# Turning queries and keys in 32x32 blocks by VectorE and transfers, instead of by TensorE, in the attention layer of a hybrid DiT

## The chip, the core and the metric

One core of one Trainium2 chip runs the whole program. The time is the device time of one execution in microseconds (us), the median of several executions. Engines are named as the profile names them: PE is TensorE (matmuls; PEld its weight loads), DVE is VectorE, ACT is ScalarE, POOL is GpSimd, SP is SyncE, which only starts transfers here.

## The reference

Two layers, 256 tokens and 256 context tokens, width 2048, float32. Layer 0 mixes by a Fourier branch; layer 1 is attention with 64 query heads on 8 kv heads of 64, a window of 128, context keys, axial rotary embedding of queries and keys, and a sink in each softmax:

```python
h = _rmsnorm(x, norm_g[i]) * (1 + scale) + shift
...
q, k, v, z = jnp.split(h @ w_in, [D_BRANCH, D_BRANCH + kvw, D_BRANCH + 2 * kvw], axis=-1)
kc, vc = jnp.split(hc @ w_in[:, D_BRANCH:D_BRANCH + 2 * kvw], 2, axis=-1)
...
q = _axial_rope(q.reshape(b, n, ATTN_Q_HEADS, ATTN_HEAD_DIM), rows, cols)
k = _axial_rope(k.reshape(b, n, ATTN_KV_HEADS, ATTN_HEAD_DIM), rows, cols)
...
s = jnp.einsum('bqhgd,bkhd->bhgqk', q, k).astype(jnp.float32) * (ATTN_HEAD_DIM ** -0.5)
...
p = jax.nn.softmax(jnp.concatenate([s, sk], axis=-1), axis=-1)[..., :-1]
return jnp.einsum('bhgqk,bkhd->bqhgd', p.astype(v.dtype), v)
...
y = jnp.moveaxis(o, 0, 1).reshape(b, n, D_BRANCH) * jax.nn.silu(z)
...
x = x + gate * (y @ w_out[i])
return _rmsnorm(x, final_g)
```

For the scores, queries and keys must stand with the 64 elements of a head in the partitions, while the projections and the rotary embedding leave them with tokens in the partitions. So they have to be turned. This turning is what the change is about.

## The kernel before

**Arithmetic.** A float32 product is made of three passes over rounded halves (`mm3`, L79 to L81): high by high, high by low, low by high. Each piece of weights, 128x1024, is cast by ACT to its high half (`w_cast`, L1119, `wh`), and DVE subtracts it from the original to get the low half (`w_low`, L1125, `wl`). The text calls the second "a low". SP's queue loads weights (L47, `raw`, 128x2048, three buffers); a load waits until the DVE has read the buffer that it takes.

**Units.** What the attention layer still has to project is cut into 142 units of 1024 weight columns: eight for the queries of each kv head, eight for its z, and fourteen for steps of the output projection. Units of the next head's queries, z and output are placed between the steps of the attention itself, so that PE has work while softmax runs.

**The attention loop.** 64 iterations, eight for each kv head; PE, DVE and ACT keep the order in which the code issues. One iteration i: DVE takes the masked maximum of the scores (`s_max`, L1215, two halves) and turns the probabilities of iteration i-1 in 32x32 blocks (`x_turn`, L1245, into `pall`); a unit goes to PE; ACT does the exponentials (L1224, L1225, `es`), then what has come due (`posts`), then the cast of a later unit; DVE and ACT divide by the sums (L1230, L1231, L1233); DVE makes a low; PE makes the scores of iteration i+1 (L1206, L1207); then come DVE's parts of what has come due (`rests`), and a second unit with its low and its cast. At every eighth iteration, PE multiplies the probabilities of the eight iterations behind it with v (`stage_o`, L1252, 256 matmuls in two halves, with a unit between them); it reads all of `pall`, so it needs the last x_turn. DVE then weights the result with z (`emit_y`, L1261), and GpSimd's queue loads v for the next head (`load_v`, L1242). A round is the stretch from one stage_o to the next; there are seven stage_o in the loop, and so six full rounds, a first one from the loop's start, and a last one.

**Turning before.** The keys, `kr`, 128 tokens x 512 by four, are turned ahead of the loop by sixteen PE transposes (L971) and copied by ACT (L973) to `kT`. The queries of heads 1 to 7: when the last unit of a head's queries is done, at the fourth iteration of the round before, ACT copies them out of PSUM (`finish_q`, L1031), GpSimd applies the rotary embedding (`roped`, L912, L917 twice, L918, for each of two blocks of tokens), and PE turns a pair of heads with four transposes (`q_turn`, L1048), one pair in the sixth iteration and the other in the seventh. An iteration later ACT casts the turned pair to its high half (`q_cast`, L1054, L1055) and DVE makes its low half (L1058, L1059), both from PSUM. A pair p2 = 0 serves the first four iterations of a head, p2 = 1 the last four. The high and low halves of a head's keys are made in the fifth iteration of the round before (`prep_kk`: ACT L1018 twice, `kkh`; GpSimd L1020 twice, `kkl`, the "k subtraction"). Of head 0, queries and keys are made ahead of the loop.

Of the kernel before, what the change touches and what calls it, by code (L numbers as in the profile page):

```python
# [10 lines left out]
F32 = mybir.dt.float32  # L11
# [18 lines left out]
def tile_dit(ctx: ExitStack, tc: tile.TileContext, a: dict, out: bass.AP):  # L30
# [888 lines left out]

    with tc.tile_pool(name="h1", reuse_waits="tile", bufs=16) as h1p:  # L920
        hx1 = []
        kT = []
        with tc.tile_pool(name="kvp", reuse_waits="tile", bufs=2) as kvp:
# [33 lines left out]
            for tb in range(4):  # L957
                t = kvp.tile([P, 512], F32, tag="v", name="v", bufs=4)
                S.copy(t, o[tb][1])
                for g in range(4):  # L960
                    nc.gpsimd.dma_start(vd[:, :, tb * 4 + g, :].rearrange("h j d -> j h d"), t[g * 32 : g * 32 + 32].rearrange("p (h d) -> p h d", d=64))
# [5 lines left out]
                kr.append(t)  # L967
            for hp in range(4):
                o = psum()
                for tb in range(4):  # L970
                    PE.transpose(o[:, tb * P : (tb + 1) * P], kr[tb][:, hp * P : (hp + 1) * P], ident)  # L971
                t = act()
                S.copy(t, o)  # L973
                kT.append(t)
# [5 lines left out]
        with tc.tile_pool(name="ye", reuse_waits="tile", bufs=6) as yep, ExitStack() as ats:  # L980
# [28 lines left out]
            now, posts, rests, turns = [-1], [], [], {}  # L1009

            def prep_kk(hk):
                kkh = at.tile([P, 512], F32R, tag="kkh", name="kkh")
                kkl = at.tile([P, 512], F32R, tag="kkl", name="kkl")
                b = (hk % 2) * 64
                src = kT[hk // 2][b : b + 64, :]
                with tc.issue_after(kk_hold[0]) if hk < 2 else nullcontext():
                    for c in (0, 64):
                        S.copy(kkh[c : c + 64, :], src)  # L1018
                for c in (0, 64):
                    (GP if hk else V).tensor_tensor(kkl[c : c + 64, :], src, kkh[b : b + 64, :].bitcast(F32), op=ALU.subtract)  # L1020
                kk[hk] = (kkh, kkl)

            def finish_q(hk, oq):
                qr = []
                for tb in range(2):
                    t = act()
                    if hk == 0:
                        roped(t, oq[tb], tb, actp, "act")
                    else:
                        t0 = act()  # L1030
                        S.copy(t0, oq[tb])  # L1031
                        roped(t, t0, tb, actp, "act", GP)
                    qr.append(t)
                if now[0] < 0:
                    prep_kk(hk)
                    for p2 in range(2):
                        defer.append(lambda p2=p2: q_cast(hk, p2, q_turn(p2, qr)))
                else:
                    posts.append((now[0] + 1, lambda: prep_kk(hk)))
                    for p2 in range(2):  # L1040
                        turns[now[0] + 2 + p2] = lambda p2=p2: (hk, p2, q_turn(p2, qr))
# [9 lines left out]
            def q_cast(hk, p2, o):  # L1051
# [10 lines left out]
                second(low)  # L1062
# [200 lines left out]
            for i in range(10):  # L1263
# [15 lines left out]
            with tc.manual_schedule(engines=engines):  # L1279
# [7 lines left out]
                for i in range(64):  # L1287
                    now[0], m = i, share[i % 8] + (i > 61 or i == 2)
# [6 lines left out]
                    run(posts)  # L1295
                    w_cast(pos[0] + 2)
# [4 lines left out]
                    run(rests)  # L1301
                    if i % 8 == 0 and i:
# [16 lines left out]
                    if i in turns:  # L1319
                        args = turns.pop(i)()  # L1320
                        posts.append((i + 1, lambda args=args: q_cast(*args)))
# [228 lines left out]
```

## Time and profile before

| What | Value |
|---|---|
| Median of 3 executions | 1769.63 us (1769.47 to 1773.46) |
| The profiled execution's own time | 1769.88 us |
| Its span, first to last instruction | 1768.1 us, granted TensorE clock 0.998 |
| Busy: PE / PEld / DVE / ACT / POOL | 99 / 84 / 78 / 50 / 10% |
| One round of the loop (1251.0 to 1311.0) | 60.0 us |
| PE transposes of the queries (L1048) / of the keys (L971) | 64 / 16 |

Times in rows are us from the span's start, then the duration; groups give the sum of busy time in us, the mean of one in ns, and the idle time ahead of them. Instructions on PE overlap, so what one costs is read from the start of one to the start of the next. A row like "[0.58 <-ACT wh L1119]" is idle time of the engine just before that instruction, and what ended it. DVE's group L1125 carries 130 lows from 1131 to 1612, about the loop (mean 1.36 us) and L1119 the casts ahead of them (mean 1.05 us). DVE and ACT instructions overlap a little with their neighbours too, by about 0.1 us.

### The profile page before, as it was taken

Reading aid. Unit: us, or ns where it says so; the run is one execution under the profiler, and the core shown is the slowest. Engines: PE = TensorE matmul, PEld = TensorE weight load, DVE = VectorE, ACT = ScalarE, POOL = GpSimd, SP = SyncE. Lnnn points to the kernel's source line nnn. Section 1 sums busy time; section 2 is a strip of 40 time slices with the busy share of each in tenths; the row PEclk is TensorE's granted clock in tenths of the full one; section 3 lists DMA queues with packets and bytes.
Section 4 is the critical chain, followed back from the end, with each engine's and each line's share of the span. In section 5 each row is a group of like instructions: output and inputs, shape, how many; then the busy total and the mean of one; then the engine's idle time right before and its main releaser. Section 6 shows DMA issues by size and latency. Waiting matters only on the chain.

```text
span 1768.1 us, 28034 instructions
## 1 busy us (share of the span) xinstructions
PE 1754.8 (99%) x10967; PEld 1480.5 (84%) x10967; DVE 1377.2 (78%) x2318; ACT 878.1 (50%) x1522; POOL 184.5 (10%) x223
## 2 busy tenths in 40 slices
PE   9999999999999999999999999999999999999998
PEld 7669999998888888888888888888888888887886
DVE  6769999978897887587986473798889888987455
ACT  6545444543222232333332352687778777876343
POOL 0001000020000010000000001133123302301000
PEclk9999999999999999999999999999999999999999
DMA  9994655476766777654566333544444444446553
GB/s 389 422 381 167 210 206 207 167 274 226 304 255 247 262 275 266 259 208 156 207 240 236 113 142 108 188 146 156 155 153 147 139 148 156 146 159 235 197 183 141
DMA packets 69108, 370.20 MB, mean 209 GB/s; under 512 B 8816, under 2 KB 11008, under 8 KB 35440
## 3 DMA queue, kind: packets, MB, share of 16 engines
q1 hardware_dynamic: 55600, 328.63, 50.5%
q0 software_dynamic: 9488, 32.95, 5.5%
q10 hardware_dynamic: 3888, 6.83, 1.1%
q8 instruction: 86, 1.41, 0.3%
q14 instruction: 46, 0.38, 0.1%
HBM read 353.16 MB, written 15.21 MB: 208 GB/s over the span
## 4 chain that ended last, share of the span: by engine, by line
PE 97%; ACT 1%; DVE 1%; DMA 0%; issue 0%; SPq 0%; DVEq 0%; ACTq 0%
PE ps L79 26%; PE ps L81 26%; PE ps L80 26%; PE ps L1177 7%; PE ps L1175 3%; PE ps L1252 3%; PE ps L347 2%; PE ps L1207 2%; PE ps L1206 2%; PE ps L1048 0%; DMA xn<-in_x 0%; PE ps L662 0%; PE ps L628 0%; PE ps L363 0%; DVE wl L1125 0%
## 5 line engine op out<-in xcount | busy, mean ns | idle before, releaser
L69 ACT CAST wh<-raw 128x1024 fp32r<-128x1024 f32 x178 | 186.9, 1053 | 402.9 <-PE ps L80 345.2
L70 DVE TENSOR_TENSOR wl<-raw,wh 128x1024 fp32r<-128x1024 f32 x178 | 219.8, 1235 | 137.9 <-ACT wh L69 137.8
L80 PE MATMUL ps<-hx,wh 128*128 128x512 f32 x700 | 272.6, 389 | 0.0
L79 PE MATMUL ps<-hx,wh 128*128 128x512 f32 x700 | 271.1, 390 | 0.0
L81 PE MATMUL ps<-hx,wl 128*128 128x512 f32 x700 | 271.1, 390 | 0.0
L1125 DVE TENSOR_TENSOR wl<-raw,wh 128x1024 fp32r<-128x1024 f32 x142 | 191.2, 1352 | 56.5 <-ACT wh L1119 56.0
L1119 ACT CAST wh<-raw 128x1024 fp32r<-128x1024 f32 x142 | 148.8, 1048 | 70.9 <-PE ps L80 58.2
L699 DVE CUSTOM_DVE_ANT_0 raw<-raw,cb 128x1024 f32<-128x1024 f32 x128 | 155.0, 1220 | 35.5 <-DMA raw<-in_adw 34.7
L79 PEld LDWEIGHTS ps<-hx,wh 128*128 128x128 f32 x700 | 131.4, 188 | 27.9 <-ACT hx L432 0.8
L81 PEld LDWEIGHTS ps<-hx,wl 128*128 128x128 f32 x700 | 131.5, 188 | 27.2
L80 PEld LDWEIGHTS ps<-hx,wh 128*128 128x128 f32 x700 | 131.5, 188 | 27.2
L699 DVE CUSTOM_DVE_ANT_0 junk<-raw,cb 128x1024 f32<-128x1024 f32 x96 | 117.2, 1221 | 27.4 <-DMA raw<-in_adw 14.1
L1177 PE MATMUL ps<-h,wh 128*128 128x512 f32 x512 | 127.3, 391 | 0.0
L79 PE MATMUL ps<-wh,h 128*128 128x512 f32 x320 | 124.9, 397 | 0.2 <-ACT h L932 0.2
L80 PE MATMUL ps<-wl,h 128*128 128x512 f32 x320 | 124.9, 390 | 0.0
L81 PE MATMUL ps<-wh,h 128*128 128x512 f32 x320 | 124.6, 391 | 0.0
L1224 ACT ACTIVATE p<-ps,mx 128x512 f32<-128x512 f32 x128 | 86.8, 683 | 52.9 <-DVE mx L1215 52.8
L1177 PEld LDWEIGHTS ps<-h,wh 128*128 128x128 f32 x512 | 94.2, 188 | 18.1
L1215 DVE CUSTOM_DVE_ANT_0 ps<-ps,mask,nsink 128x512 f32<-128x512 f32 x128 | 91.1, 752 | 0.5
L80 PE MATMUL ps<-act,wh 128*128 128x512 f32 x234 | 91.0, 389 | 0.0
L81 PE MATMUL ps<-act,wl 128*128 128x512 f32 x234 | 90.3, 390 | 0.3 <-DVE wl L70 0.3
L79 PE MATMUL ps<-act,wh 128*128 128x512 f32 x234 | 89.7, 389 | 0.0
(362 smaller groups left out, 3959.8 us busy)
## 6 DMA issues: line engine op xcount, KB each, us to landing
raw<-in_adw SPq DMA_DIRECT2D x64, 1024.0 KB, 4.9
raw<-in_wz SPq DMA_DIRECT2D x58, 1024.0 KB, 4.8
raw<-in_awp SPq DMA_DIRECT2D x32, 1024.0 KB, 12.4
raw<-in_wo SPq DMA_DIRECT2D x32, 1024.0 KB, 4.8
raw<-in_wq SPq DMA_DIRECT2D x32, 1024.0 KB, 4.7
raw<-in_wu SPq DMA_DIRECT2D x25, 1016.0 KB, 5.0
raw<-in_wo1b SPq DMA_DIRECT2D x16, 1024.0 KB, 4.8
act<-in_xT POOLq DMA_DIRECT2D x32, 256.0 KB, 5.6
```

The costliest lines, as they stand in the source:

```text
L69: cast[0] = S.copy(h, t[:, i * 1024 : (i + 1) * 1024]).ins
L70: V.tensor_tensor(l, t[:, i * 1024 : (i + 1) * 1024], h.bitcast(F32), op=ALU.subtract)
L79: PE.matmul(o, wh, xh, start=start, stop=False)
L80: PE.matmul(o, wh, xl, start=False, stop=False)
L81: return PE.matmul(o, wl, xh, start=False, stop=stop).ins
L699: V.tensor_tensor_reduce(junk if s == 0 and i < 3 else wf, wf, cb[:, s], 1.0, 0.0, ALU.mult, ALU.add, acc[:, i, kh, fg * 2 + f, s : s + 1])
L1119: cast[0] = S.copy(h, t[:, i * 1024 : (i + 1) * 1024]).ins
L1125: V.tensor_tensor(ready[n][1], ready[n][2], ready[n][0].bitcast(F32), op=ALU.subtract)
L1175: PE.matmul(o[0][:, 0:N], wl[:, q], hx1[k][:, 0:N], start=False, stop=False)
L1177: PE.matmul(o[0], wh[:, q], hx1[k], start=k == 0, stop=k == KT - 1)
L1215: V.tensor_tensor_reduce(so[tb], so[tb], mask[:, tb, :], -0.125, nsink[:, i : i + 1], ALU.add, ALU.min, mx[:, tb : tb + 1])
L1224: S.activation(pt[:, tb, :], so[tb], AF.Exp, bias=mx[:, tb : tb + 1], scale=-1.0, accum_out=sm[:, tb : tb + 1])
```

## The change

The turning leaves PE, except for head 0's queries.

- **Keys**: DVE turns `kr` in 32x32 blocks into `kt` (four instructions of 128x512), four transfers started by ACT write it to a scratch in memory, `kd`, each block row to its place, and four transfers started by GpSimd read it back as `kT`, now with the heads' elements in the partitions. Within `kT` the tokens stand in another order of blocks; `prep_kk` reads it through a view that puts them right.
- **Queries of heads 1 to 7**: ACT copies per pair of heads (four of 128x256 in place of two of 128x512); GpSimd's rotary embedding works per pair (six instructions, 128x512 and four of 128x128, chained one behind the other) instead of per block of tokens. `q_blocks` then turns a pair by one DVE block transpose of 128x512, writes it by four transfers of 64 KB to `qd` and reads it back by four. The first pair goes by SP's queue, in the fifth iteration of the round before; its cast stands in the seventh. The second goes by GpSimd's queue, from the end of the eighth iteration; its cast stands in the third iteration of the head itself, ahead of the fifth, which uses it. Casts and lows of queries read SBUF now, not PSUM.
- **Keys' high and low halves**: from the fifth iteration of the round before to the second, right behind the exponentials and ahead of the weight cast.
- One unit that stood in the loop at i == 2 is done ahead of the loop.

In the order of DVE, at the fifth iteration (between the rows of the maximum), before (L1125 is a low, L1189 a part of z):

```order
L1230 TENSOR_TENSOR sm<-sm,es 128x2
L1231 RECIPROCAL sm<-sm 128x2
L1125 TENSOR_TENSOR wl<-raw,wh 128x1024
L1189 TENSOR_TENSOR zs<-ps,zs 128x256
L1125 TENSOR_TENSOR wl<-raw,wh 128x1024
L1215 ISA ps,mx<-ps,mask,nsink 128x512
```

and after (the same lines are now L1266, L1267, L1161, L1225, L1251; L1072 is the block transpose of the first pair):

```order
L1266 TENSOR_TENSOR sm<-sm,es 128x2
L1267 RECIPROCAL sm<-sm 128x2
L1161 TENSOR_TENSOR wl<-raw,wh 128x1024
L1225 TENSOR_TENSOR zs<-ps,zs 128x256
L1072 STREAM_TRANSPOSE act<-act 128x2x8x32
L1161 TENSOR_TENSOR wl<-raw,wh 128x1024
L1251 ISA ps,mx<-ps,mask,nsink 128x512
```

The first pair's transpose now stands ahead of the second low of the iteration. At the end of the eighth iteration of the round, DVE before, with the lows of the second pair of queries (L1058, L1059):

```order
L1125 TENSOR_TENSOR wl<-raw,wh 128x1024
L1191 SCALAR_TENSOR_TENSOR th<-th,zs 128x256
L1189 TENSOR_TENSOR zs<-ps,zs 128x256
L1058 TENSOR_TENSOR qa<-ps,qa 64x512
L1059 TENSOR_TENSOR qb<-ps,qb 64x512
L1125 TENSOR_TENSOR wl<-raw,wh 128x1024
L1215 ISA ps,mx<-ps,mask,nsink 128x512
```

and after (L1281 is x_turn, the last one that stage_o needs):

```order
L1161 TENSOR_TENSOR wl<-raw,wh 128x1024
L1227 SCALAR_TENSOR_TENSOR th<-th,zs 128x256
L1225 TENSOR_TENSOR zs<-ps,zs 128x256
L1161 TENSOR_TENSOR wl<-raw,wh 128x1024
L1072 STREAM_TRANSPOSE act<-act 128x2x8x32
L1251 ISA ps,mx<-ps,mask,nsink 128x512
L1251 ISA mx 128x1
L1251 ISA ps,mx<-ps,mask,nsink 128x512
L1251 ISA mx 128x1
L1281 STREAM_TRANSPOSE pall<-p 128x2x16x32
```

The query lows have left this place (to the third iteration of the next round), and the second pair's transpose stands ahead of the maximum and the x_turn. On ACT, the second and third iterations of a round, before:

```order
L1224 ACTIVATE p,sm<-ps,mx 128x512 x2
L1225 ACTIVATE es<-mx,sink 128x2
L1119 CAST wh<-raw 128x1024
L1233 ACTIVATE p<-p,sm 128x512 x2
L1119 CAST wh<-raw 128x1024
L1224 ACTIVATE p,sm<-ps,mx 128x512 x2
L1225 ACTIVATE es<-mx,sink 128x2
L1119 CAST wh<-raw 128x1024
```

and after (L1260, L1261, L1155, L1269 are the same lines; L1044 is the cast of the keys, L1090 and L1091 that of a pair of queries):

```order
L1260 ACTIVATE p,sm<-ps,mx 128x512 x2
L1261 ACTIVATE es<-mx,sink 128x2
L1044 CAST kkh<-act 64x512 x2
L1155 CAST wh<-raw 128x1024
L1269 ACTIVATE p<-p,sm 128x512 x2
L1155 CAST wh<-raw 128x1024
L1260 ACTIVATE p,sm<-ps,mx 128x512 x2
L1261 ACTIVATE es<-mx,sink 128x2
L1090 CAST qa<-act 64x512
L1091 CAST qb<-act 64x512
L1155 CAST wh<-raw 128x1024
```

Two casts of keys stand ahead of the weight cast in the second iteration, and two of queries in the third. The diff, cut to its core:

```diff
+    pool_end = [None]
+    def pooled(f):
+        with tc.issue_after(pool_end[0]) if pool_end[0] else nullcontext():
+            pool_end[0] = f().ins
+
+    def roped_pair(dst, src):
...
+        pooled(lambda: GP.tensor_tensor(v(dst), v(src), rope[:, 0].unsqueeze(2).broadcast_to([P, 2, 4, 64]), op=ALU.mult))
+        for tb in range(2):
+            for u in range(2):
+                pooled(lambda: GP.tensor_tensor(t4[:, tb, :, :, u, :], s4[:, tb, :, :, 1 - u, :], sn[:, tb, :, u, :].unsqueeze(1).broadcast_to([P, 4, 2, 16]), op=ALU.mult))
+        pooled(lambda: GP.tensor_tensor(dst, dst, t2, op=ALU.add))
+
+    def block_out(d, t, x, g, q):
+        return q.dma_start(d.rearrange("(b j) (g x) -> j b g x", j=32, g=4)[:, :, g, :], t[g * 32 : g * 32 + 32].rearrange("p (b x) -> p b x", x=x))
+
+            for tb in range(4):
+                V.transpose(kt[:, :, tb, :], kr[tb].rearrange("p (b j) -> p b j", j=32))
+            for g in range(4):
+                block_out(kd, kt.rearrange("p b t i -> p (b t i)"), 128, g, nc.scalar)
             for hp in range(4):
-                o = psum()
-                for tb in range(4):
-                    PE.transpose(o[:, tb * P : (tb + 1) * P], kr[tb][:, hp * P : (hp + 1) * P], ident)
                 t = act()
-                S.copy(t, o)
+                nc.gpsimd.dma_start(t, kd[hp * P : (hp + 1) * P, :])
                 kT.append(t)
...
+                ts = []
+                for p2 in range(2):
+                    t0, t = act(), act()
+                    for tb in range(2):
+                        S.copy(t0[:, tb * N : (tb + 1) * N], oq[tb][:, p2 * N : (p2 + 1) * N])
+                    roped_pair(t, t0)
+                    ts.append((t, t0))
+                n = now[0]
+                middle[n + 1] = lambda: q_blocks(hk, 0, *ts[0], nc.sync)
+                turns[n + 4] = lambda: q_blocks(hk, 1, *ts[1], nc.gpsimd)
+                posts.append((n + 3, lambda: second(q_cast(hk, 0, ts[0][0]))))
+                posts.append((n + 7, lambda: second(q_cast(hk, 1, ts[1][0]))))
+
+            def q_blocks(hk, p2, t, t0, q):
+                V.transpose(t0.rearrange("p (b t i) -> p t b i", b=8, t=2), t.rearrange("p (t b j) -> p t b j", t=2, b=8))
+                for g in range(4):
+                    block_out(qd[hk, p2], t0, 64, g, q)
+                for r in range(2):
+                    for tb in range(2):
+                        q.dma_start(t[:, (r * 2 + tb) * P : (r * 2 + tb + 1) * P].rearrange("p (g i) -> p g i", g=4), qd[hk, p2].rearrange("(r p) (g t i) -> p r t g i", p=P, g=4, t=2)[:, r, tb])
...
-            for i in range(10):
+            for i in range(11):
...
-                    now[0], m = i, share[i % 8] + (i > 61 or i == 2)
+                    now[0], m = i, share[i % 8] + (i > 61)
...
                     run(posts)
+                    if i % 8 == 1 and i < 56:
+                        prep_kk(i // 8 + 1)
                     w_cast(pos[0] + 2)
                     s_norm(i)
                     w_low(pos[0] + 1)
                     if i + 1 < 64:
                         s_mm(i + 1)
                     run(rests)
+                    if i in middle:
+                        middle.pop(i)()
```

More of the change, by code (lines that the diff above doesn't have):

```diff
@@ L1008, in o1_step @@
                     mm3(os_[tb], yh[k][:, tb * P : (tb + 1) * P], yh[k][:, N + tb * P : N + (tb + 1) * P], wh, wl, k == 0, k == NB - 1)
-            now, posts, rests, turns = [-1], [], [], {}
+            now, posts, rests, turns, middle = [-1], [], [], {}, {}
             def prep_kk(hk):
@@ L1014, in prep_kk @@
                 b = (hk % 2) * 64
-                src = kT[hk // 2][b : b + 64, :]
+                src = kT[hk // 2][b : b + 64, :].rearrange("p (g t i) -> p t g i", g=4, t=4)
+                kh, kl = (x.rearrange("p (t g i) -> p t g i", t=4, g=4) for x in (kkh, kkl))
                 with tc.issue_after(kk_hold[0]) if hk < 2 else nullcontext():
                     for c in (0, 64):
-                        S.copy(kkh[c : c + 64, :], src)
+                        S.copy(kh[c : c + 64], src)
@@ L1019, in prep_kk @@
                 for c in (0, 64):
-                    (GP if hk else V).tensor_tensor(kkl[c : c + 64, :], src, kkh[b : b + 64, :].bitcast(F32), op=ALU.subtract)
+                    (GP if hk else V).tensor_tensor(kl[c : c + 64], src, kh[b : b + 64].bitcast(F32), op=ALU.subtract)
                 kk[hk] = (kkh, kkl)
             def finish_q(hk, oq):
[L1024 to L1033, printed above, removed]
@@ L1034, in finish_q @@
-                if now[0] < 0:
+                if hk == 0:
+                    qr = [act() for _ in range(2)]
+                    for tb in range(2):
+                        roped(qr[tb], oq[tb], tb, actp, "act")
                     prep_kk(hk)
                     for p2 in range(2):
[L1037 to L1041, printed above, removed]
+                        defer.append(lambda p2=p2: q_cast(hk, p2, q_turn(p2, qr))())
+                    return
@@ L1061, in q_cast @@
                 qq[hk, p2] = (qa, qb)
-                second(low)
+                return low
             def units():
@@ L1319, in tile_dit @@
                     if i in turns:
[L1320 to L1321 removed]
+                        turns.pop(i)()
                 x_turn(63)
```

8 lines of the change are left out of this document (added).

## The prediction

> **What bounds the kernel now.** The page first: how full TensorE is, and whose work ends last.
>
> ```profile
> span 1768.1 us, 28034 instructions
> PE 1754.8 (99%) x10967; PEld 1480.5 (84%) x10967; DVE 1377.2 (78%) x2318; ACT 878.1 (50%) x1522; POOL 184.5 (10%) x223
> PE 97%; ACT 1%; DVE 1%; DMA 0%; issue 0%; SPq 0%; DVEq 0%; ACTq 0%
> ```
>
> Read alone, this says that every matmul taken away is time gained: PE is 97% of the chain. But 78% for VectorE is an average, and the change gives VectorE work inside the attention loop. So I cut out one round of eight iterations, from the first half of stage_o of one head (1251.0) to that of the next (1311.0), and split it where DVE's idle time ends.
>
> ```profile
> 1251.00:1261.40 10.40, 10.40 (x270) 8.05 (x270) 4.08 (x7) 3.72 (x6) 0.00 (x0) 1.00 0.38 114
> 1261.40:1282.50 21.10, 21.10 (x108) 18.08 (x109) 19.65 (x42) 16.80 (x35) 7.90 (x9) 1.00 0.49 170
> 1282.50:1311.00 28.50, 28.50 (x149) 24.02 (x147) 28.13 (x48) 25.19 (x51) 8.26 (x6) 1.00 0.42 148
> 1251.00:1311.00 60.00, 60.00 (x525) 50.15 (x524) 51.86 (x95) 45.71 (x91) 16.16 (x14) 1.00 0.43 150
> ```
>
> After the length come PE, PEld, DVE, ACT, POOL. DVE rests only while PE does stage_o (4.08 of 10.40); afterwards it is busy 47.78 of 49.60 us, and PE all of them. The timelines of DVE and PE show how the round closes: stage_o needs `pall`, which DVE's x_turn writes.
>
> ```profile
> 1249.75 1.24 DVE L1245 STREAM_TRANSPOSE pall<-p 128x1024 f32<-128x1024 f32 x1
> 1251.02 3.71 PE L1252 MATMUL ps<-pall,vr 32*64 32x256 f32 x128
> 1261.39 1.67 DVE L1261 SCALAR_TENSOR_TENSOR act<-ps,th 128x128 f32<-128x128 f32 x8 [1.58 <-PE ps L1252]
> 1309.81 1.24 DVE L1245 STREAM_TRANSPOSE pall<-p 128x1024 f32<-128x1024 f32 x1
> 1310.98 3.81 PE L1252 MATMUL ps<-pall,vr 32*64 32x256 f32 x128
> ```
>
> x_turn ends at 1250.99 and 1311.05, stage_o starts at 1251.02 and 1310.98: no slack at either end. DVE starts when stage_o is done (1261.39) and is back for the next one 49.66 us later; PE's own work takes exactly as long. PE and DVE are both critical in each round. What PE saves there is worth nothing unless DVE's round gets shorter too, and what DVE gains in length is paid in full. Unused on DVE there is only:
>
> ```profile
> 1267.10 1.22 DVE L1125 TENSOR_TENSOR wl<-raw,wh 128x1024 fp32r<-128x1024 f32 x1 [0.58 <-ACT wh L1119]
> 1277.92 1.82 DVE L1125 TENSOR_TENSOR wl<-raw,wh 128x1024 fp32r<-128x1024 f32 x1 [0.43 <-ACT wh L1119]
> 1282.48 0.53 DVE L1230 TENSOR_TENSOR sm<-sm,es 128x2 f32<-128x2 f32 x1 [0.24 <-ACT es L1225]
> ```
>
> **Part by part. PE transposes, removed.** PE's timeline around four q transposes and around twelve of the sixteen k transposes:
>
> ```profile
> 1300.20 0.39 PE L81 MATMUL ps<-wh,h 128*128 128x512 f32 x1
> 1300.43 0.60 PE L1048 MATMUL ps<-ident,act 128*128 128x128 f32 x4
> 1300.78 0.48 PE L79 MATMUL ps<-wh,h 128*128 128x512 f32 x1
> 1301.10 0.40 PE L80 MATMUL ps<-wl,h 128*128 128x512 f32 x1
> 1106.36 1.47 PE L971 MATMUL ps<-ident,kr 128*128 128x128 f32 x12
> 1107.59 0.48 PE L81 MATMUL ps<-wh,h 128*128 128x512 f32 x1
> ```
>
> From start to start a matmul takes 0.23. The four take 0.35 and the matmul behind them 0.32: 0.35 + 0.09 = 0.44. Twelve take 1.23 + 0.09; with another four, k costs 1.75. Seven heads have two groups of four: 0.88 a head, 6.2 in all. At full worth: -7.9.
>
> **DVE, two block transposes a head.** Of 128x512, half of this group's 1.24: 0.62 each, 1.24 a head, both between stage_o's end and the last x_turn.
>
> ```profile
> L1245 DVE STREAM_TRANSPOSE pall<-p 128x1024 f32<-128x1024 f32 x64 | 79.2, 1237 | 0.0
> L1018 ACT CAST kkh<-act 64x512 fp32r<-64x512 f32 x16 | 9.9, 621 | 0.2
> L1031 ACT COPY act<-ps 128x512 f32<-128x512 f32 x14 | 7.5, 588 | 0.0
> L1186 ACT COPY zs<-ps 128x256 f32<-128x256 f32 x32 | 11.6, 362 | 0.0
> ```
>
> **ACT, the casts of k moved.** Two of 0.621 move to the iteration after stage_o, ahead of the very wh cast for which DVE already waits 0.58 (row 1267.10). That wait becomes 0.58 + 1.24 = 1.82. At their old place the DVE had other work, so nothing comes back. The second pair's q casts move to the next iteration but one after stage_o: there DVE has its next two lows of weights and q in hand, so nothing is counted. Four copies of 0.362 for two of 0.588: 0.27 more of ACT, in an iteration with 0.43 of DVE waiting; this keeps part of that wait alive.
>
> **DVE's round** thus grows by 1.24 + 1.24 = 2.48. If the other two waits (0.43 + 0.24) are swallowed, by 1.8; if not, by 2.5. I take 1.8, the lower end, since a DVE that runs late finds ACT's results lying ready.
>
> **GpSimd beside DVE.** Its k subtraction (the same two instructions) moves too. Before, timeline of both engines:
>
> ```profile
> 1283.13 1.64 DVE L1125 TENSOR_TENSOR wl<-raw,wh 128x1024 fp32r<-128x1024 f32 x1
> 1283.66 4.51 POOL L918 TENSOR_TENSOR act<-act,rt 128x512 f32<-128x512 f32 x2
> 1285.09 1.92 DVE L1125 TENSOR_TENSOR wl<-raw,wh 128x1024 fp32r<-128x1024 f32 x1
> 1288.25 2.65 POOL L1020 TENSOR_TENSOR kkl<-act,kkh 64x512 fp32r<-64x512 f32 x2
> 1289.72 2.26 DVE L1125 TENSOR_TENSOR wl<-raw,wh 128x1024 fp32r<-128x1024 f32 x1
> ```
>
> A low beside the rope's last sums takes 0.70 longer than one with DVE to itself (1.22, row 1267.10), one beside the k subtraction 1.04 longer over 1.18 us together (0.88 per us). After, the casts end at about 1267.3 in this round's clock, the two subtractions run to 1269.9, the low starts at 1268.3: 1.6 us beside them, at 0.88 enough for 1.04 again. The rope's six pieces a pair have the elements of the old ones. Taken at no change; the bounds are -1.04 a head, if the subtractions fall into DVE's idle time, and +0.6, if the low stands still for all 1.6.
>
> The row beside the k subtraction can be read in another way: the low of 1289.72 starts to move only when the second subtraction has ended (1288.25 + 2.65 = 1290.90) and then needs its usual time (to 1291.98). The Trainium skill (SBUF — State Buffer, Who interferes with whom) says just that: a VectorE instruction with two SBUF inputs and a GpSimd instruction that reads SBUF share one port pair, and the later one blocks until the other has ended. What that makes of the new place is rival (b).
>
> **Transfers.** Nearest rows, and the consumer of the first pair:
>
> ```profile
> vd<-v POOLq DMA_DIRECT2D x16, 64.0 KB, 3.0
> raw<-in_wq SPq DMA_DIRECT2D x32, 1024.0 KB, 4.7
> vr<-vd POOLq DMA_DIRECT2D x32, 128.0 KB, 4.4
> L961 POOL DMA_DIRECT2D vd<-v x16 | 9.2, 585 | 88.1 <-ACT v L959 87.2 <-DMA vd<-v 0.9
> 1284.84 0.33 SPq L47 DMA_DIRECT2D raw<-in_wq  x1
> 1292.04 0.33 SPq L47 DMA_DIRECT2D raw<-in_wq  x1
> 1296.33 0.58 ACT L1054 CAST qa<-ps 64x512 fp32r<-64x512 f32 x1
> ```
>
> First pair: the transpose stands ahead of the low of 1285.09, so it ends near 1285.7; the cast is due at 1296.3: 10.6 us. SP needs 4 x 0.33, a write of 64 KB 3.0, 4 x 0.33, a read 3.0: 8.6, hidden. With reads in smaller runs (4.4) and 1.7 more, since the weight load issued at 1284.84 is on its way for 4.7: 11.7, not hidden; that is a rival. On SP the weight loads behind the block transfers wait for DVE's transpose and for the writes; the last read is issued near 1291.3 (1285.7 + 1.3 + 3.0 + 1.3), the next weight load was due at 1292.04, when its buffer comes free: no cost, and one of a few us only if that load is late by more than its tile's lead. Second pair: GpSimd's 8 x 0.585 + 2 x 3.0 = 10.7, against some 20 from its transpose at the round's end (near 1308) to its cast in the second iteration of the next (beyond 1327, row 1267.10 one round later); behind it on GpSimd are the v loads, which wait for stage_o anyway, and k's subtraction an iteration later. k, once: four block transposes of 0.62 and transfers ahead of the loop, where several units of q matmuls lie between; nothing to 3 us, taken at nothing.
>
> **The first round** differs, as DVE's waits from the loop's start to the first stage_o show:
>
> ```profile
> DVE wl L1125 <- ACT wh L1119: 2.3, 2, 1.8
> DVE qa L1058 <- ACT qb L1055: 1.7, 1, 1.7
> DVE sm L1230 <- ACT es L1225: 1.2, 2, 1.0
> ```
>
> 5.2 us stand there to take the 2.48, so PE's 0.88 is realised: -0.9. The unit that moves from i == 2 ahead of the loop is the same work elsewhere: 0. The last round turns nothing: 0.
>
> **Sum.** -1.75 (k) - 0.9 (first round) + 6 x 1.8 = +8.2. The profiled execution took 1769.88 by the table of times (span 1768.1 and 1.8 around it), 0.25 above the median: 1769.9 + 8.2 = 1778.1, against the median 1777.8; I say 1778. With 2.5 a round it is 1782.
>
> **The rivals.** (a) *GpSimd's drag on DVE goes, and PE's saving stands.* Then DVE's round has to fit PE's new one, 60.0 - 0.88 = 59.1: 2.48 + 0.88 = 3.36 to be freed. The four lows quoted beside GpSimd's work (1.82, 1.64, 1.92, 2.26) stand 2.76 above four of 1.22, and the two waits give 0.67: 3.43, just enough, if the chained pieces of 128x128 leave DVE alone and the k subtraction falls into DVE's wait after stage_o. It gives -1.75 - 0.9 - 6 x 0.88 = -7.9: 1762, and it decides at a DVE round of 59.1. For it: the drag is as large as what the change adds. Against: the same elements pass through the same GpSimd beside the same lows. 0.16. (b) *The k subtraction costs less at its new place.* If engines wait for whole instructions, the low that starts at 1268.3 meets the first of the two subtractions (1267.3 to 1268.6), waits 0.3 for its end and goes ahead of the second: 0.74 less than before, 1.8 - 0.74 = 1.06 a round, -2.65 + 6.4 = +3.7, 1773.6. If it is freed altogether, 1.8 - 1.04 = 0.76: 1771.8. The other way round, behind both, it is +0.6 a round and 1781.6. For it: the row of 1289.72. Against: the meeting hangs on 0.3 us, and comes out differently each time. By the rule of the Trainium skill named above this case, one side or the other, is the one to expect. 0.23. (c) *First pair late*: at 11.7 us ACT stands at the q cast for 1.1, the wh cast behind it and DVE's low with it: 6 x 1.1 = 6.6 more, 1785; at 12.2, 1788. For it: weight loads of 1024 KB share the queue. Against: DVE's round is longer by then, and so is the time to the cast. 0.18. That the transposes stay on PE is excluded by the instruction order.
>
> **How the numbers follow.** A measurement here tells apart some 0.3%, 5.3 us: faster below 1764.3, slower above 1774.9. The forecast (1775 to 1783, the far side of (b) in it) has 0.43, (c) 0.18: slower 0.61. (b) is no change that could be measured: 0.23. (a) is faster: 0.16. The range takes in the forecast's bounds and (c) up to 1788, and (b) and the upper part of (a) down to 1763: 1763 to 1788.
>
> **What would show it.** Right: rounds of 61.8 to 62.5 us between stage_o starts; PE waiting 1 to 2 us there for DVE; DVE's wait for the wh cast after stage_o 1.8; no wait of ACT's q casts on DMA. Wrong: rounds of 60 or less; a stage_o without wait; DVE transposes far from 0.62; lows of 1.2 where GpSimd works; ACT waiting for `act` from the queues.

## The result, and the profile after

| | Median | Lowest to highest | n |
|---|---|---|---|
| Before | 1769.60 us | 1769.38 to 1773.46 | 6 |
| Changed | 1779.37 us | 1778.03 to 1785.65 | 6 |

The ratio is 1.0056, 95% interval 1.0039 to 1.0072: slower by 9.8 us, where 8.2 were forecast. The size came out; of the steps behind it, several were wrong, in opposite directions.

The page of the changed kernel, to be read against that of before:

```profile
span 1783.7 us, 28178 instructions
PE 1759.8 (99%) x10895; PEld 1478.1 (83%) x10895; DVE 1381.3 (77%) x2336; ACT 878.5 (49%) x1532; POOL 231.9 (13%) x311
PE 82%; DVE 7%; ACT 6%; DMA 3%; issue 2%; SPq 1%; ACTq 0%; DVEq 0%; POOLq 0%
```

PE has 72 instructions less and still counts as 99% busy; what tells is the chain of work that ended last, where DVE and ACT have 13% (2% before) and the transfers appear. The profiled execution is the slowest of the six. Against the trace of before it lies like this: first stage_o 0.3 us earlier, the six rounds 10.3 longer (mean 61.76 against 60.04, from the starts of stage_o), the last round 0.9 longer (62.0 against 61.07), and some 5 us in the output part behind the loop. Those last 5 belong to this execution, not to the change; PE's timeline there:

```profile
1634.41 0.50 PE L81 MATMUL ps<-wh,act 128*128 128x512 f32 x1 [3.21 <-issue]
1634.75 0.39 PE L79 MATMUL ps<-wh,act 128*128 128x512 f32 x1
...
1636.18 0.63 PE L81 MATMUL ps<-wh,act 128*128 128x512 f32 x1
```

PE stood for 3.21 without anything in the trace to wait for, and then ran for a while at 0.63 a matmul instead of 0.39. The five other executions took 1778.0 to 1780.5, so by their times they had no such stop.

**The second iteration of a round**, where the keys' casts went: ACT, GpSimd and DVE in two successive rounds.

```profile
1268.39 1.25 ACT L1044 CAST kkh<-act 64x512 fp32r<-64x512 f32 x2
1269.72 3.54 POOL L1046 TENSOR_TENSOR kkl<-act,kkh 64x512 fp32r<-64x512 f32 x2 [3.71 <-ACT kkh L1044]
1270.75 1.35 DVE L1161 TENSOR_TENSOR wl<-raw,wh 128x1024 fp32r<-128x1024 f32 x1 [1.99 <-ACT wh L1155]
...
1330.60 1.25 ACT L1044 CAST kkh<-act 64x512 fp32r<-64x512 f32 x2
1331.29 2.63 POOL L1046 TENSOR_TENSOR kkl<-act,kkh 64x512 fp32r<-64x512 f32 x2 [2.96 <-ACT kkh L1044]
1332.96 2.05 DVE L1161 TENSOR_TENSOR wl<-raw,wh 128x1024 fp32r<-128x1024 f32 x1 [1.86 <-ACT wh L1155]
```

DVE's wait for the weight cast is 1.99 and 1.86; 1.82 was forecast from 0.58 + 1.24. The low behind it takes 1.35 in one round and 2.05 in the next, not 2.26 each time: that is rival (b). DVE's other two waits (0.43 and 0.24 before), which the sum counted as swallowed, read like this in the first of the two rounds:

```profile
1283.16 1.70 DVE L1161 TENSOR_TENSOR wl<-raw,wh 128x1024 fp32r<-128x1024 f32 x1 [0.54 <-ACT wh L1155]
1309.19 0.16 DVE L1266 TENSOR_TENSOR sm<-sm,es 128x2 f32<-128x2 f32 x1 [0.28 <-ACT es L1261]
```

The first is still at its place; the second has gone from the fifth iteration, and one of its size stands at the end of the eighth.

**The turn, its transfers, the cast of the first pair**, in the fifth and seventh iteration, and what GpSimd does beside the low ahead of it:

```profile
1350.66 1.30 POOL L931 TENSOR_TENSOR act<-act,rope 128x512 f32<-128x512 f32 x1
1350.84 2.20 DVE L1161 TENSOR_TENSOR wl<-raw,wh 128x1024 fp32r<-128x1024 f32 x1
1353.10 1.22 PE L1211 MATMUL ps<-h,wl 128*128 128x256 f32 x8 [0.80 <-DVE wl L1161]
1353.30 0.70 DVE L1072 STREAM_TRANSPOSE act<-act 128x512 f32<-128x512 f32 x1
1353.43 0.33 SPq L47 DMA_DIRECT2D raw<-in_wq  x1
1354.02 3.17 SPq L941 DMA_DIRECT2D qd<-act  x4
1360.09 2.55 SPq L1077 DMA_DIRECT2D act<-qd  x4
1364.84 0.62 ACT L1090 CAST qa<-act 64x512 fp32r<-64x512 f32 x1 [1.45 <-issue]
```

The weight load got onto SP's queue 0.6 ahead of the writes; issuing them takes 3.17 here (1.85 to 3.17 over the seven first pairs) instead of 4 x 0.33, and issuing the reads 2.55 instead of 1.3. From the transpose's end to the end of the last read's issue pass 8.6, and ACT waits 1.45 at the cast. The groups of the transfers, and ACT's waits in the loop:

```profile
qd<-act SPq DMA_DIRECT2D x28, 64.0 KB, 4.7
act<-qd SPq DMA_DIRECT2D x28, 64.0 KB, 2.5
...
ACT qa L1090 <- issue: 5.0, 4, 1.9
ACT qa L1090 <- DMA act<-qd: 4.2, 3, 2.3
```

All seven first pairs wait, 9.2 us in all; that "issue" stands for the transfers too is shown below by a kernel without them (E4). That is rival (c); it was priced at 6.6 us, and E4 measures 4.4.

**Where PE pays** (its waits from the loop's start on, then DVE, PE and PEld at one stage_o):

```profile
PE ps L1211 <- DVE wl L1161: 4.3, 6, 0.8
PE ps L81 <- issue: 3.2, 1, 3.2
PE ps L80 <- DVE wl L1161: 2.7, 4, 1.5
...
1314.33 1.24 DVE L1281 STREAM_TRANSPOSE pall<-p 128x1024 f32<-128x1024 f32 x1
1314.36 4.95 PE L1288 MATMUL ps<-pall,vr 32*64 32x256 f32 x128
1315.33 3.52 PEld L1288 LDWEIGHTS ps<-pall,vr 32*64 32x64 f32 x122 [0.49 <-ACT p L1260]
```

The stage's first half takes 4.95 instead of 3.81: it begins 1.2 before the last x_turn ends (1314.33 + 1.24 = 1315.57), and its own loads (PEld) come to a stop and go on only at 1315.33. Besides, PE waits up to 0.8 in six rounds at a unit of z (L1211), whose low comes late in the fifth iteration.

### The profile page after: what moved, and what is told of

Same layout as the page of the kernel before. It is cut to its first block, busy times and chain, and to the rows that moved or that the text cites. A ratio compares the mean times of both kernels' runs of the same rounds, so it can differ in the third digit from the quotient of the medians.

```text
span 1783.7 us, 28178 instructions
## 1 busy us (share of the span) xinstructions
PE 1759.8 (99%) x10895; PEld 1478.1 (83%) x10895; DVE 1381.3 (77%) x2336; ACT 878.5 (49%) x1532; POOL 231.9 (13%) x311
## 4 chain that ended last, share of the span: by engine, by line
PE 82%; DVE 7%; ACT 6%; DMA 3%; issue 2%; SPq 1%; ACTq 0%; DVEq 0%; POOLq 0%
PE ps L79 24%; PE ps L80 23%; PE ps L81 23%; PE ps L1288 4%; DVE wl L1161 3%; PE ps L1213 2%; ACT wh L1155 2%; PE ps L347 2%; ACT p L1260 1%; DVE ps L1251 1%; PE ps L1211 1%; DMA kd<-kt 1%; DMA qd<-act 1%; PE ps L1242 1%; PE ps L1243 1%
## 5 line engine op out<-in xcount | busy, mean ns | idle before, releaser
L70 DVE TENSOR_TENSOR wl<-raw,wh 128x1024 fp32r<-128x1024 f32 x178 | 220.4, 1239 | 136.2 <-ACT wh L69 136.0
L80 PE MATMUL ps<-hx,wh 128*128 128x512 f32 x700 | 272.3, 389 | 0.0
L1161 DVE TENSOR_TENSOR wl<-raw,wh 128x1024 fp32r<-128x1024 f32 x142 | 186.4, 1314 | 62.8 <-ACT wh L1155 60.6
L1155 ACT CAST wh<-raw 128x1024 fp32r<-128x1024 f32 x142 | 148.7, 1049 | 55.4 <-PE ps L80 49.9
L80 PEld LDWEIGHTS ps<-hx,wh 128*128 128x128 f32 x700 | 131.4, 188 | 27.3
L80 PE MATMUL ps<-wl,h 128*128 128x512 f32 x320 | 125.3, 392 | 2.8 <-DVE wl L1161 2.7
L1260 ACT ACTIVATE p<-ps,mx 128x512 f32<-128x512 f32 x128 | 86.9, 684 | 64.2 <-DVE mx L1251 64.0
L80 PE MATMUL ps<-act,wh 128*128 128x512 f32 x234 | 90.9, 389 | 0.0
L1251 DVE CUSTOM_DVE_ANT_0 ps<-ps,mask,nsink 128x512 f32<-128x512 f32 x128 | 90.7, 749 | 0.0
```

Source lines behind the costliest of these rows:

```text
L70: V.tensor_tensor(l, t[:, i * 1024 : (i + 1) * 1024], h.bitcast(F32), op=ALU.subtract)
L80: PE.matmul(o, wh, xl, start=False, stop=False)
L1155: cast[0] = S.copy(h, t[:, i * 1024 : (i + 1) * 1024]).ins
L1161: V.tensor_tensor(ready[n][1], ready[n][2], ready[n][0].bitcast(F32), op=ALU.subtract)
L1251: V.tensor_tensor_reduce(so[tb], so[tb], mask[:, tb, :], -0.125, nsink[:, i : i + 1], ALU.add, ALU.min, mx[:, tb : tb + 1])
L1260: S.activation(pt[:, tb, :], so[tb], AF.Exp, bias=mx[:, tb : tb + 1], scale=-1.0, accum_out=sm[:, tb : tb + 1])
```

## The experiments

Times are medians; the kernel before stood at 1769.7 to 1770.0 in the runs beside them, with intervals of some 0.1% either way. "Round" is the mean of the six rounds in the run's trace (from starts of stage_o).

| Kernel | us | Round |
|---|---|---|
| Before | 1769.6 | 60.04 |
| Changed | 1779.4 | 61.76 |
| E1 keys' casts back | 1774.9 | 60.82 |
| E2 before, keys' casts moved | 1770.5 | 60.13 |
| E3 no DVE turn | 1769.7 | 60.18 |
| E4 no first-pair transfers | 1775.0 | 60.96 |
| E5 as E4, needed cast last | 1773.9 | 60.68 |
| E6 before, keys turned by blocks | 1769.8 | 60.02 |
| E7 nothing added to the round | 1762.5 | 59.04 |
| E8 keys' casts in stage_o | 1770.4 | 60.18 |
| E9 as E8, first pair on PE | 1764.7 | 59.47 |
| E10 as E8, turn ahead of the low | 1761.7 | 59.04 |
| E11 as E8, no first-pair transfers | 1764.6 | 59.32 |
| E12 before, keys' casts in stage_o | 1769.1 | 59.98 |

The theory (D): DVE's round sets the time, and the change makes it longer by the wait behind the keys' casts and by two turns. The rival (Q): the price is the first pair's transfers.

**E1, the keys' casts back in the fifth iteration.**

```diff
-                    if i % 8 == 1 and i < 56:
+                    if i % 8 == 4 and i < 56:
                         prep_kk(i // 8 + 1)
```

> The changed kernel with one part undone: the casts and subtractions of the keys' halves stand in the fifth iteration of a round again, not in the second. Theory D (DVE's round sets the time; the casts ahead of the weight cast cost it 1.28 a round, from 0.58 to 1.86 of waiting): six rounds shorter by 0.8 to 1.3, 1771 to 1774.5. Rival Q (the price is the first pair's transfers, for which ACT waits 9.2 us in the profile of the changed kernel, half in q casts): no change, 1778 to 1780.

1774.93, ratio to before 1.0034 (1.0022 to 1.0046): 4.4 less than the changed kernel, at the upper edge of theory D's range. But it isn't clean. ACT's waits show that the transfers became punctual as well:

```profile
ACT qa L1090 <- issue: 1.1, 2, 0.6
```

The low beside the subtractions, now again between the turn and the q cast, takes 2.32, which presumably gives the transfers the time they lack. The 4.4 is not the price of the casts alone.

**E2, the keys' casts moved, on the kernel before.** The same two lines added to the kernel before, and the old call taken out.

> The kernel before with this one part of the change alone: the casts and subtractions of the keys' halves in the second iteration of a round, ahead of the weight cast; all turning stays on PE. Theory D: DVE's round longer by 1.28, less what the waits of 0.43 and 0.24 take: 6 x 0.6 to 6 x 1.3 more, 1773 to 1777.5, without any transfer. Rival Q: no change, 1769.6.

1770.54, ratio 1.0005 (0.9996 to 1.0013): a miss for theory D as it was put. The wait is there, but nearly nothing is lost. GpSimd and DVE in two successive rounds, and two more lows of the first of them, say why:

```profile
1267.38 3.53 POOL L1020 TENSOR_TENSOR kkl<-act,kkh 64x512 fp32r<-64x512 f32 x2 [3.78 <-ACT kkh L1018]
1268.35 1.41 DVE L1124 TENSOR_TENSOR wl<-raw,wh 128x1024 fp32r<-128x1024 f32 x1 [1.99 <-ACT wh L1118]
1279.15 1.81 DVE L1124 TENSOR_TENSOR wl<-raw,wh 128x1024 fp32r<-128x1024 f32 x1 [0.43 <-ACT wh L1118]
1285.56 1.42 DVE L1124 TENSOR_TENSOR wl<-raw,wh 128x1024 fp32r<-128x1024 f32 x1
...
1326.58 2.65 POOL L1020 TENSOR_TENSOR kkl<-act,kkh 64x512 fp32r<-64x512 f32 x2 [0.78 <-ACT kkh L1018]
1328.25 2.06 DVE L1124 TENSOR_TENSOR wl<-raw,wh 128x1024 fp32r<-128x1024 f32 x1 [1.87 <-ACT wh L1118]
```

The low lost 1.04 at its old place beside the subtractions, and loses 0.19 or 0.84 at the new one. The rounds here read 59.96, 59.95, 60.38, 59.95, 60.58, 59.96: the two long ones are 0.4 and 0.6 longer, and the one of the rows, 60.38, has the longer low. What pays for the wait, 1.41 longer in the first of the two rounds, is not the 0.67 that DVE had spare: 0.43 of it still stands at 1279.15. It is the low at the old place (0.85 less on balance), and the fifth iteration, where the low that stood beside the rope's last sums (1.92 in the row of 1285.09 before) takes 1.42, since GpSimd starts these sums only at 1285.86.

**E3, no block transpose of queries** (the transfers take the unturned tile).

```diff
-                V.transpose(t0.rearrange("p (b t i) -> p t b i", b=8, t=2), t.rearrange("p (t b j) -> p t b j", t=2, b=8))
                 for g in range(4):
-                    block_out(qd[hk, p2], t0, 64, g, q)
+                    block_out(qd[hk, p2], t, 64, g, q)
```

> The changed kernel without DVE's block transposes of the queries of heads 1 to 7: the transfers take the unturned tile, so scores of these heads are other numbers. Theory D: 2 x 0.63 less DVE a round, 6 x 1.0 to 6 x 1.26 less, 1771.5 to 1773.5. Rival Q: the transfers start 0.63 earlier and are still waited for, at most 6 x 0.6 less, 1775.5 to 1778.

1769.70, ratio 1.0002 (0.9993 to 1.001): 9.7 less, more than either theory gave. The round is shorter by 1.58, where the turns are 1.26. But this run isn't clean either: without the turn the writes get onto SP's queue ahead of the weight load, and no cast of a first pair waits any more. SP and ACT in one round:

```profile
1283.31 1.82 SPq L941 DMA_DIRECT2D qd<-act  x4
1285.70 0.35 SPq L47 DMA_DIRECT2D raw<-in_wq  x1
1295.11 0.61 ACT L1089 CAST qa<-act 64x512 fp32r<-64x512 f32 x1
```

So the 9.7 hold the price of the late transfers too. The next run takes that price alone, 4.4; the difference, 5.3 or 0.78 a round (60.96 to 60.18), is what the two turns cost beside the moved casts.

**E4, no first-pair transfers** (the casts read what DVE turned).

```diff
+                if p2 == 0:
+                    return
                 for g in range(4):
...
-                posts.append((n + 3, lambda: second(q_cast(hk, 0, ts[0][0]))))
+                posts.append((n + 3, lambda: second(q_cast(hk, 0, ts[0][1]))))
```

> The changed kernel without the first pair's eight transfers on SyncE's queue: DVE still turns the pair, and the casts read the turned blocks directly, so half the scores of heads 1 to 7 are other numbers. Theory D: the wait for the transfers lies in ACT's spare time, 1776.5 to 1779.5. Rival Q: 6 to 7 x 1.3 us of ACT's waiting go, and with them DVE's: 1770 to 1772.

1775.00, ratio 1.0029 (1.0018 to 1.004): 4.4 less, between the two. ACT's waits at the q casts, 9.2 in the changed kernel, are gone, those called "issue" with them. So the transfers cost 0.8 a round (61.76 to 60.96), and rival Q holds about half of the loss. Its rounds read 59.92, 60.95, 61.50, 60.93, 61.50, 60.94: from the second on, the alternation again.

**E5, the cast that the subtraction needs comes last**, on E4.

```diff
-                    for c in (0, 64):
+                    for c in (64 - b, b):
                         S.copy(kh[c : c + 64], src)
```

> The kernel without the first pair's transfers (half the scores of heads 1 to 7 are other numbers), and the two casts of the keys' halves in such an order that the one which GpSimd's subtraction reads always comes second. Without that order its rounds alternate between 60.9 and 61.5. Theory B (a whole subtraction blocks a whole low: where the subtractions start one cast earlier, the low meets the second one and is 0.83 longer, otherwise it slips in between them and is 0.19 longer): all rounds 60.9, 1773.4 against 1775.0. Rival: the alternation has to do with which pair of heads shares a tile of keys, and stays: 1775.

The rounds are 59.32, 60.94, 60.97, 60.95, 60.94, 60.94: the alternation is gone, by an exchange of two casts. The first round, 0.6 shorter than E4's, fits: its low takes 1.46 where E4's takes 2.05. 1773.90 against 1775.00. Half of the keys of a tile stand in partitions 0 to 63 and half in 64 to 127; the subtractions read the one cast of their own half and start behind it, 0.6 earlier or later. Started later, they let the low in between them; started earlier, the first of them is over when the low comes, and it waits for the second (in the changed kernel it comes at 1332.96, and the pair ends at 1333.92). Theory B is shown, and with it rival (b).

**E6, only the keys by blocks.** The kernel before with `kd`, the four DVE transposes, the eight transfers and the reordering view; queries as before.

> The kernel before with the keys turned by DVE and transfers, the queries on PE as before. If the transfers are hidden: 1.75 less, 1767.9. If the write to memory, 9.1 us in the profile of the changed kernel, makes head 0's casts late, as there: PE waits about 1.6 once, 1769.5.

1769.84, ratio 1.0004 (0.9995 to 1.0012): the 1.75 is not there. ACT and PE ahead of the loop:

```profile
ACT kkh L1026 <- DMA act<-kd: 2.2, 1, 2.2
PE ps L1056 <- DVE act L918: 1.6, 2, 1.3
```

The keys come back 2.2 late, DVE's work for head 0 moves with them, and PE stands 1.6. In the changed kernel it was 3.4 late and PE stood 1.5 (of 2.7 in the row L80 above); the write to memory took 9.1 there, 7.1 here. That the saving is always lost doesn't follow: in the traces of E3, E4, E7, E8 and E10, which have the rest of the change ahead of the loop as well, PE waits at most 0.4 there, and the second half of the first stage_o starts 1.5 to 2.3 earlier than in the kernel before (1195.4 to 1196.2 against 1197.67).

**E7, nothing added to the round**: no turn, no first-pair transfers, and the keys' casts moved into stage_o (of head 1 they stay in the second iteration):

```diff
                         stage_o(oo, 1)
+                        if i < 56:
+                            prep_kk(i // 8 + 1)
                         w_low(pos[0] + 1)
```

> The changed kernel without DVE's block transposes of queries, without the first pair's transfers, and with the keys' casts and subtractions moved to stage_o, where ACT and DVE stand idle (scores of heads 1 to 7 are other numbers). Theory D says that everything that the change adds to the round is then gone, and PE's 0.88 a round shows: rounds of 59.1 to 59.3, 1762 to 1764. Rival P: rounds stay at 60, 1768 to 1769; then the loop is held by something else than these three.

1762.53, ratio 0.9957 (0.9944 to 0.9969), and every round is 59.04. PE's saving exists, 1.0 a round; three things keep it back: the turns, the casts' place, the transfers.

**E8, complete again, only the keys' casts in stage_o** (the same edit, nothing left out).

> The changed kernel, complete, with the casts and subtractions of the keys' halves during stage_o, behind its second half in ACT's order and ahead of the cast for which ACT waits there. Theory D: the 1.28 of waiting goes, and so does the low's 0.19 or 0.83 beside the subtractions; the turns and the late first pair stay: rounds of 60.5 to 60.9, 1772 to 1774.5. Rival: the place in the round doesn't matter, 1778 to 1779.

1770.43, ratio 1.0003 (0.9994 to 1.0013): 9 less than the changed kernel for the place of four instructions, more than expected (1772 at best). In stage_o, ACT had stood 4.4 ahead of the weight cast and DVE 4.7; now the casts and most of the subtractions lie in that time. What is left against E7 is 8, and ACT still waits for the first pair:

```profile
ACT qa L1090 <- issue: 4.8, 4, 2.0
ACT qa L1090 <- DMA act<-qd: 4.3, 3, 1.8
```

**E9, E8 with the first pair turned by PE again** (four transposes from the pair's tile, in the sixth iteration).

> The changed kernel, complete, with the keys' casts and subtractions in stage_o and the first pair of each head turned by PE again, the second by DVE and transfers. DVE is given one turn of 0.63 a round and relieved of the low's 1.04 beside the subtractions, so Theory D expects PE to set the round: 59.04 (the rounds with nothing added) + 0.44 = 59.5; with the keys' late transfers 1766 to 1767.5, under both kernels. Rival: one turn still costs its 0.63 and the rounds stay at 60: 1769 to 1770.

1764.69, ratio 0.9972 (0.9962 to 0.9982), 1.3 below the expected range; rounds of 59.47. One turn on DVE is fully covered, and PE pays 0.43 for its four transposes, as priced.

**E10, E8 with the first pair's turn ahead of the first low.**

```diff
                     s_norm(i)
+                    if i in middle:
+                        middle.pop(i)()
                     w_low(pos[0] + 1)
...
                     run(rests)
-                    if i in middle:
-                        middle.pop(i)()
```

> The changed kernel, complete, with the keys' casts and subtractions in stage_o and the first pair's block transpose ahead of the first low of the fifth iteration, not of the second: its transfers start some 2.4 earlier and are ready when the casts are due. If the late transfers are what is left (2 us of waiting at the q casts in four heads): rounds of 59.5 to 59.8, 1766 to 1768. Rival: the low behind the transpose, for which PE waits 0.8 at this place already in the changed kernel, is late by 0.63 more, and nothing is gained: 1770 to 1771.

1761.65, ratio 0.9956 (0.9942 to 0.9969): the best, complete, 4 below the expected range, 8 us under the kernel before and as fast as E7, which leaves out the turns and the first pair's transfers. GpSimd, DVE, SP and ACT at the place:

```profile
1340.01 1.30 POOL L931 TENSOR_TENSOR act<-act,rope 128x512 f32<-128x512 f32 x1
1340.18 0.69 DVE L1072 STREAM_TRANSPOSE act<-act 128x512 f32<-128x512 f32 x1
1340.80 1.58 DVE L1161 TENSOR_TENSOR wl<-raw,wh 128x1024 fp32r<-128x1024 f32 x1
1341.26 1.90 SPq L941 DMA_DIRECT2D qd<-act  x4
1343.27 1.94 SPq L47 DMA_DIRECT2D raw<-in_wq  x1
1346.08 2.59 SPq L1077 DMA_DIRECT2D act<-qd  x4
1351.86 0.61 ACT L1090 CAST qa<-act 64x512 fp32r<-64x512 f32 x1
```

Two things are seen. The writes now go ahead of the weight load, in all seven rounds, and the cast has no wait. They land in 1.8 (median of the trace), where those of the changed kernel, behind a load, took 4.7. They also start earlier: 10.6 ahead of the cast (1341.26 to 1351.86), against 9.4 ahead of the time at which ACT was ready for it (1354.02 to 1364.84 - 1.45). What each of the two is worth was not separated; in E1 the load was still ahead (landing 4.5), and more time alone took most of the wait away. And the turn costs nothing: in the changed kernel the low ended 1.08 behind GpSimd's instruction (1351.96 to 1353.04), having stood beside it; here it ends 1.07 behind it (1341.31 to 1342.38) although the turn went ahead. The turn lies in the time in which the low would have waited for GpSimd. The rival of this run, a later low, is refuted.

**E11, E8 without the first pair's transfers**, the edit of E4.

> The kernel with the keys' casts and subtractions in stage_o, without the first pair's transfers on SyncE's queue (both pairs are still turned by DVE; half the scores of heads 1 to 7 are other numbers). What is left of its distance to 1762.5 is the price of the two turns. Theory D: 2 x 0.63 less 0.7 of spare time, rounds of 59.3 to 59.7, 1764 to 1766.5. Rival (the turns alone cost all of the 8 us): 1769 to 1770.5.

1764.57, ratio 0.9973 (0.9964 to 0.9982). So of the 8 us between E8 and E7, the transfers hold 5.9 and the turns, at this place, 2.0. Its rounds are 59.04 and 59.46, longer than E10's.

**E12, the kernel before with the keys' casts in stage_o.**

> The kernel before with the keys' casts and subtractions (from head 2 on) in stage_o; all turning on PE. DVE's round loses the 1.04 that a low stood beside the subtractions, PE's work stays. Theory D says that both engines fill the round of 60.0, so DVE's gain alone is worth nothing: 1769.3 to 1770. Rival (DVE alone sets the round before): 6 x 1.0 less, 1763.5.

1769.12, ratio 0.9997 (0.9988 to 1.0006). DVE's round lost its 1.04, the time stayed. DVE relieved alone is worth nothing. PE relieved alone was not run. The nearest is E3 beside E2: both have the keys' casts moved, no turn on DVE and no cast waiting for transfers of queries; in E3 PE's transposes of queries are gone as well, and its rounds are 60.18 against 60.13. As the two differ in the rotary embedding and in the place of q casts too, this is an indication only.

## Why the prediction was right, and where it was not

- *"PE and DVE are both critical in each round"*: held, as far as it was tried. E12 takes work from DVE alone and gains nothing; E3 has less work on PE than E2 and is not faster in its rounds; the change takes work from PE, adds to DVE, and loses; E10 takes the same from PE with DVE's additions covered and gains it all.
- *Rounds of 61.8 to 62.5*: 61.76 in the mean, just below; the single ones read 61.50, 62.34, 62.46, 61.39, 61.82, 61.07. The sum for the rounds, 6 x 1.8 = 10.8, came out at 10.3, but its inside was wrong three times:
- *"GpSimd beside DVE ... taken at no change"*: mis-sized. It was 1.04 a round before, 0.13 or 0.83 after, 0.56 a round to the good in the mean. Failed was the price by overlapping time (0.88 per us); what holds is whole instruction against whole instruction, in an order that changes with the head. The prediction had this as rival (b), and as a rule of the Trainium skill, and didn't take it for the likeliest.
- *The first pair's transfers: "8.6, hidden"*: failed. ACT waits for every one of them, which the prediction had named as a sign that it is wrong. The step took 0.33 for each issue on SP and 3.0 for the landing; with the weight load just ahead it was up to 3.17 and 2.55 for four issues, and 4.7 for the landing of the write. E4 puts it at 4.4 us.
- *"If the other two waits (0.43 + 0.24) are swallowed, by 1.8"*: failed for the larger. 0.54 still stands in its place (1283.16), and 0.56 in the trace of E4, where no transfer is late, so lateness of DVE did not swallow it.
- *The wait behind the casts, 1.82*: right (1.86 and 1.99). That it is also lost was right only because nothing else was spare by then: E2 has the wait and hardly the loss.
- *The turns, 0.62 each*: 0.70 in the group, 0.63 from start to start. Right in size; in E10 they cost nothing, in E11 0.28 a round, and between E4 and E3 0.78, depending on what stands beside.
- *k: -1.75, "taken at nothing"* for its transfers: in the profiled execution most of it was repaid at the loop's start, where PE stood 1.5 because the keys came back late. E6 has it alone: no gain. In E3, E4, E7, E8 and E10 PE waits at most 0.4 there, so the loss is not the same in every kernel; what decides it was not tried.
- *The first round, -0.9, and the last, 0*: the first stage_o started 0.3 earlier instead of 2.65, and its second half 0.6 later than before (1198.31 against 1197.67). The last round's 0.9 belongs to the round ahead of it: the stage_o that opens it starts early and halts, so that from its start to its second half it is 7.64 (1561.10 to 1568.74) against 6.72 (1551.08 to 1557.80); from there to the next stage_o it is 54.36 against 54.35. So the 0 for the last round was right.
- *PE waiting 1 to 2 us at stage_o*: about 1.1 there; PE also waits, up to 0.8, at a unit of z in the fifth iteration, which the prediction didn't name.

So the mechanism was right in the main, and the number owes something to luck, to errors that cancel: about 3.4 us too much for the subtractions (6 x 0.56), about 4.4 too little for the transfers, up to 2.6 too little for the wait that stayed (6 x 0.43), and in the profiled execution about 1.5 too much for k's gain. These four alone would put the forecast some 5 us too low; it was 1.6 too low (8.2 for 9.8). Where the rest went stays open.

The effects don't add up one by one either. E1, E3 and E4 remove 4.4, 9.7 and 4.4 from a loss of 9.8 against before, but the first two contain part or all of the transfers' price. Taken off one behind the other, down to E7, the time without any of them, the transfers are 4.4 (E4), the casts' place 10.4 (to E11) and the turns 2.0 (to E7); or, with the turns before the casts, 4.4, 5.3 (to E3) and 7.2 (to E7). Both make 16.8: the whole is firm, a part's price hangs on what else is still there. The right zero was not the kernel before, but 1762.

## What to carry to other kernels

Where two engines fill the same round, price a change against what the relieved engine could reach, not against the time before; and find out where the loaded engine stands idle, because moving the same four instructions from behind the exponentials into stage_o took 9 us off the changed kernel (E8), and with them there PE has no wait in the rounds of E10. Put an instruction with one input where its neighbour would have to wait for another engine anyway. A transfer that goes and comes back through a queue of large loads needs more time than its own rows say: its writes landed in 1.8 ahead of the next load (E3, E10) and in 4.7 behind it (the changed kernel, E8).

## What the runs showed of the hardware

- A DVE subtraction of two SBUF operands and a GpSimd one wait for each other whole. In the changed kernel the low of 1332.96 ends 1.09 behind GpSimd's pair (1333.92), and the pair of 1269.72 is stretched from 2.63 to 3.54 when the low gets in between. This is the rule of the Trainium skill that the prediction weighed (SBUF — State Buffer, Who interferes with whom), and these rows agree with it.
- DVE's block transpose, with one input, isn't slowed by GpSimd: 0.69 beside L931 (1340.18 in E10), 0.70 in the group of the changed kernel, and 0.70 at 1312.39 there, where GpSimd did no arithmetic. The same section of the Trainium skill says that a VectorE instruction with at most one SBUF input, outside the modes that use both ports, doesn't contend, and these rows agree with it.
- After PE's 3.2 us without work behind the loop, matmuls take 0.63, and the windows of that stretch of the changed kernel show a granted clock of 0.63:

```profile
1630.80:1634.40 3.60, 0.40 (x2) 0.00 (x0) 2.79 (x12) 2.80 (x6) 1.06 (x2) 1.00 0.70 264
1634.40:1638.80 4.40, 4.39 (x13) 3.44 (x14) 0.03 (x1) 1.16 (x2) 0.00 (x0) 0.63 0.71 289
```

The trace of E11 shows the same stop, of 2.94, and that execution took 1769.72 against its median of 1764.57. What PE waits for there stays open.
